# Three paddings in SBUF that move the operands of matrix products to multiples of 128 bytes

## The chip, the cores and the metric

The kernel is one program on one NeuronCore of a Trainium2 chip. The metric is the device time of one execution in microseconds, as the median of several runs. The engines are named as in the profile: PE (TensorE, matrix products; PEld is its loading of the stationary operand), DVE (VectorE), ACT (ScalarE), POOL (GpSimd) and SP (SyncE, which here only issues DMAs).

## The reference

One layer of a hybrid decoder: a token mixer with two parallel branches, then an MLP, both with RMS norm and residual, then a final RMS norm. The sequence has 1024 rows, the model width is 1024, all in float32. Cut to what matters:

```python
h = rms_norm(x, norm_mix)
xa, ga, q, f, v, g, m_a, m_b = split(h @ w_in)             # w_in: 1024 x 8192
xa = causal_depthwise_conv(xa, conv_w, conv_b)             # four taps
y_a = rg_lru(xa, w_r, b_r, w_i, b_i, lam) * gelu(ga)       # four blocks of 256 x 256 for each gate, then a scan
o = rms_norm(hgrn2_chunkwise(silu(q), k, log_f, v), hg_norm)   # 8 heads of 128
y = sigmoid(m_a) * y_a + sigmoid(m_b) * (o * silu(g))
x = x + y @ w_out                                          # 1024 x 1024
h = rms_norm(x, norm_mlp)
x = x + square(relu(h @ w_up)) @ w_down                    # 1024 x 4096, 4096 x 1024
out = rms_norm(x, norm_final)
```

## The kernel before

All large products run in fp32r, and each is made of three (`mm3`, L113): both operands are split into a high part H, rounded by ACT (L76), and the rest L, which DVE subtracts (L77); then H x H, H x L and L x H are accumulated in one PSUM bank. `PE.matmul(o, a, b)` takes `a` as the stationary operand (128 columns, loaded into the array) and `b` as the moving one (here up to 512 columns, read from SBUF while the product runs). In the profile's rows a product stands as `out<-moving,stationary`. L115, L116 and L117 are the three products of `mm3`.

The work goes in this order:

- Mixer. The sequence is cut into two halves of T = 512 rows (`c`), the width into four pairs of heads (`p`). For each of the 8 combinations: projections `v`, `xa`, `q`, `f`, `g`, `mb`, `ga`, `ma` (`project`, L270: 48 products of 512 columns with the normalised rows hT as the moving operand; `project_v`, L282: products of 256 columns with the weights moving); `conv` (L296), which writes the projection xa behind three carried columns into a tile `xp` and splits its result into xcH and xcL; `rg_lru` (L326) with 24 products per pair for its two gates, xcH and xcL moving; `hgrn` (L381), a chain of elementwise work on DVE with small fp32 products of 32, 48, 64 and 128 columns between; `gates` (L561). `out_proj` (L599) follows for the first half.
- Second norm (L686), with the output projection of the second half between its parts. Its results, in seven combinations (a scheme with seven instead of eight block products), are the tiles h2 (`hop`, L680): t1, n2, T3, T4, B11, B21, B22, each H and L.
- First half of the MLP (`hidden`, L804): 16 quads of 256 hidden columns, each in seven steps (`PLAN`) of 12 products of 512 columns, h2 moving, weights stationary. X, Y and Z are the banks that the steps accumulate into. ACT copies the bank of the first three steps out (L819), DVE and ACT finish the others (L822 to L827). The results u are split, combined, and most of them stored in HBM.
- Second half of the MLP (from L936): 8 rounds of two quads, 168 products of 512 columns per round. The weights move (the even quad from the pools w1 and wp, the odd one from late_w1 and late_w); the stationary operand is u (from ust and late_u). DVE adds the banks to the residual `acc` (L963). The last round is finished tile by tile with the final norm (`finish`, L917).

The order of instructions on each engine is fixed when the program is built; semaphores hold it. SBUF is handed out by pools: a pool takes its tiles one after the other, each rounded up to 32 bytes in a partition. Pools of the left side grow upwards from the small constants; those opened with `side="right"` grow downwards from the upper end: first `pad` (L673), one tile that nobody reads, then the four h2 pools, and, after these are closed, late_u, acc0, late_w, late_w1, late_raw and acc1. The mixer's pool `mix` lies on the left. Its tiles in order: the masks, scar, scT, g1, g2, on, xc, f, tmp, kT, v, then xp (two buffers, L300), xcH, xcL, q1, kk, h, rw, ri, rr, dd, seg, qa, hssq (two buffers, L518), sn and hrs. A tile that takes over bytes of a closed pool waits for the instructions that used the tile before.

Of the kernel before, what the change touches and what calls it, by code (L numbers as in the profile page):

```python
# [10 lines left out]
F32 = mybir.dt.float32  # L11
# [7 lines left out]
P = 128  # L19
D = 1024  # L20
S = 1024
T = 512
# [19 lines left out]
def trunk(ctx: ExitStack, tc: tile.TileContext, x, wts, mlp, pv, gains, mask_f, mask_u, out):  # L42
# [8 lines left out]
    def opened(name, **how):  # L51
        cm = tc.tile_pool(name=name, bufs=1, reuse_waits="tile", **how)
        return cm.__enter__(), lambda: cm.__exit__(None, None, None)
# [21 lines left out]
    def split(src, h, lo):  # L75
        keep(A.copy(h, src))  # L76
        keep(V.tensor_tensor(out=lo, in0=src, in1=h.bitcast(F32), op=ALU.subtract))  # L77
# [92 lines left out]
    def mt(tag, name, shape=(P, T), dt=F32, bufs=1):  # L170
        return m.tile(list(shape), dt, tag=tag, name=name, bufs=bufs)
# [98 lines left out]
    def project(c, name):  # L270

        pp = [bank("pj", f"pj_{name}_{s}") for s in range(2)]
        for half in range(2):
            wh, wl = next_w()
            for k in range(4):
                hh, hl = kt(hT[c], 4 * half + k)
                for s in range(2):
                    cols = slice(k * 256 + s * P, k * 256 + (s + 1) * P)
                    mm3(pp[s], wh[:, cols], wl[:, cols], hh, hl, half == 0 and k == 0, half == 1 and k == 3)
        return pp  # L280
# [15 lines left out]
    def conv(c, p, pp):  # L296
        xc = mt("xc", f"xc{c}{p}", (P, 2, T))
        for s in range(2):
            u = 2 * p + s
            xp = mt("xp", f"xp{c}{u}", (P, T + 3), bufs=2)  # L300
            V.tensor_copy(xp[:, 0:3], xcar[:, u, :])
            A.copy(xp[:, 3 : T + 3], pp[s])
            A.activation(
                xc[:, s, :],
                pp[s],
                AF.Identity,
                bias=pvt[:, PV_CB + u : PV_CB + u + 1],
                scale=pvt[:, PV_CW + 24 + u : PV_CW + 25 + u],
            )
            for j in range(3):  # L310
                V.scalar_tensor_tensor(  # L311
                    xc[:, s, :],
                    xp[:, j : j + T],
                    pvt[:, PV_CW + 8 * j + u : PV_CW + 8 * j + u + 1],
                    xc[:, s, :],
                    op0=ALU.mult,
                    op1=ALU.add,
                )
            if c + 1 < NC:
                G.tensor_copy(xcar[:, u, :], xp[:, T : T + 3])  # L320
        xh = mt("xcH", f"xcH{c}{p}", (P, 2, T), F32R)
        xl = mt("xcL", f"xcL{c}{p}", (P, 2, T), F32R)
        split(xc, xh, xl)
        return xc, xh, xl
# [43 lines left out]
    def f_of(c, p, pp):  # L368
        ff = mt("f", f"f{c}{p}", (P, 2 * T))
        kk = mt("kk", f"kk{c}{p}", (P, 2 * T))  # L370
        for s in range(2):
            u = 2 * p + s
            f, k = ff[:, s * T : (s + 1) * T], kk[:, s * T : (s + 1) * T]
            A.activation(f, pp[s], AF.Sigmoid)
            A.activation(k, pp[s], AF.Sigmoid, scale=-1.0)
            V.tensor_scalar(f, f, omlb[:, u : u + 1], lb[:, u : u + 1], op0=ALU.mult, op1=ALU.add)
            V.tensor_scalar(k, k, omlb[:, u : u + 1], None, op0=ALU.mult)
        V.tensor_scalar(ff, ff, F_MIN, 1.0, op0=ALU.max, op1=ALU.min)
        return ff, kk

    def hgrn(c, p, q1, f, kk, v):  # L381

        nm = f"{c}{p}"
# [131 lines left out]


        on = mt("on", f"on{nm}", (P, 8, P))
        ssq = mt("hssq", f"hssq{nm}", (P, 8), bufs=2)  # L518
        nkv = 3 if c + 1 == NC else 4
        pos = []  # L520
        for s in range(2):
            u = 2 * p + s
# [103 lines left out]
    for c in range(NC):  # L626
        if c == 0:
            first_norm(0)
            mu32 = small_inputs()
        else:  # L630
            out_proj(0, ys, res0, done0, lambda: first_norm(1))
        ys = a2_set(a2y, f"y{c}")
        for p in range(NPAIR):
            v = project_v(c, f"{c}{p}")
            px = project(c, f"xa{c}{p}")
            if c == 0 and p == 0:
                parameters()
                tc.keep_in_program_order(V.tensor_copy(mu, mu32.to_broadcast([P, 7, 8, 32])))
            xc3 = conv(c, p, px)
            q1 = q_of(c, p, project(c, f"q{c}{p}"))  # L640
            f, kk = f_of(c, p, project(c, f"f{c}{p}"))
            with tc.high_priority(300):
                h = rg_lru(c, p, *xc3)
            on = hgrn(c, p, q1, f, kk, v)
            gates(c, p, h, on, ys)
# [25 lines left out]


    pad, close_pad = opened("pad", side="right")  # L673
    pad.tile([P, 8], F32, tag="pad", name="pad")

    h2p = [opened(f"h2{i}", side="right") for i in range(4)]
    HOME = {"T4": 0, "B22": 0, "T3": 0, "B21": 1, "n2": 2, "t1": 2, "B11": 3}
# [371 lines left out]
```

## Time and profile before

| | before |
|---|---|
| median of 3 runs | 1631.38 us (1631.27 to 1631.52) |
| profiled execution | span 1628.7 us from the first to the last instruction; a time of its own beside the span is not recorded for it |
| median of the runs less the span | 2.7 us |
| PE busy | 1584.9 us, 97%, 9240 products |
| DVE busy | 1212.7 us, 74% |
| ACT busy | 764.4 us, 47% |
| mean granted TensorE clock | 0.996 |
| DMA | 246.51 MB, mean 151 GB/s |

How to read the profile: it is one execution. A row of the order of time has the start in us from the begin of the span, the duration in us, the engine, the line, the operation, and what it writes and reads; what stands in square brackets is how long the engine sat idle before, and who ended that. The printed durations of products overlap, since the next one starts while the last one still runs through the array; what a product costs in a dense row is the distance between two starts. A row of the waits names who waited for whom, the sum in us, how many times, and the longest.

### The profile page before, as it was taken

How to read it: one execution, taken by the hardware profiler on the slowest of the kernel's cores; microseconds unless marked ns; L12 is line 12 of the kernel's file. 1: busy time of each engine (PE TensorE's matmuls, PEld its weight loads, DVE VectorE, ACT ScalarE, POOL GpSimd, SP SyncE). 2: the span in 40 equal slices, each digit the busy share in tenths (PEclk: the TensorE clock that was granted, in tenths of full speed). 3: DMA queues.
4: the chain of work that ended last, by engine and by line, in shares of the span. 5: the costliest groups of instructions: out<-in, count | busy, mean ns of one | idle time of the engine just before them, and what ended most of it. 6: DMA issues, size and time to landing. Idle time of an engine off the chain costs nothing.

```text
span 1628.7 us, 23177 instructions
## 1 busy us (share of the span) xinstructions
PE 1584.9 (97%) x9240; PEld 1303.1 (80%) x9240; DVE 1212.7 (74%) x1751; ACT 764.4 (47%) x1186; POOL 65.8 (4%) x99
## 2 busy tenths in 40 slices
PE   7999999999999999999999997999999999999998
PEld 6788788788788788787787876888878878888886
DVE  5975956848764865848759688977777888888876
ACT  4643545435442544436434566766776731222113
POOL 0010100100100000100100100000000000000000
PEclk9999999999999999999999998999999999999999
DMA  6212212122243222222122352666656575666652
GB/s 237 91 66 91 91 66 103 66 91 91 80 167 136 86 78 90 80 78 101 69 91 91 117 207 104 250 246 250 235 233 248 222 269 228 251 244 251 254 203 104
DMA packets 57996, 246.51 MB, mean 151 GB/s; under 512 B 6688, under 2 KB 6816, under 8 KB 47136
## 3 DMA queue, kind: packets, MB, share of 16 engines
q1 hardware_dynamic: 56304, 239.27, 39.3%
q10 hardware_dynamic: 1584, 5.77, 1.0%
q8 instruction: 72, 1.18, 0.3%
q14 instruction: 36, 0.29, 0.1%
HBM read 185.24 MB, written 59.77 MB: 150 GB/s over the span
## 4 chain that ended last, share of the span: by engine, by line
PE 80%; DVE 16%; DMA 2%; issue 1%; ACT 1%; POOL 0%; DVEq 0%; POOLq 0%; SPq 0%; ACTq 0%
PE dX L115 3%; PE uX L115 3%; PE uX L117 3%; PE uX L116 3%; PE dX L116 3%; PE dX L117 3%; DVE wL L77 2%; PE pj_ga L117 2%; PE pj_ga L116 2%; PE pj_ga L115 2%; PE pj_f L117 2%; PE pv L115 2%; PE pv L117 2%; PE pv L116 2%; PE pj_ma L117 2%; PE pj_ma L116 2%
## 5 line engine op out<-in xcount | busy, mean ns | idle before, releaser
L77 DVE TENSOR_TENSOR wL<-raw,wH 128x1024 fp32r<-128x1024 f32 x160 | 194.3, 1214 | 150.0 <-ACT wH L76 145.8
L76 ACT CAST wH<-raw 128x1024 fp32r<-128x1024 f32 x160 | 167.9, 1050 | 168.1 <-issue 66.4
L963 DVE TENSOR_TENSOR acc<-acc,dX 128x512 f32<-128x512 f32 x128 | 85.2, 684 | 31.2 <-PE dX L117 30.1
L76 ACT CAST wA<-q 128x512 fp32r<-128x512 f32 x32 | 19.8, 621 | 129.6 <-PE dX L117 103.7
L963 DVE TENSOR_TENSOR acc<-acc,dY 128x512 f32<-128x512 f32 x64 | 43.6, 686 | 17.3 <-PE dY L117 15.7
L345 DVE RECIPROCAL rr<-rr 128x512 f32<-128x512 f32 x16 | 53.5, 3347 | 0.0
L823 ACT ACTIVATE b<-b 128x512 f32<-128x512 f32 x48 | 30.2, 631 | 38.6 <-DVE b L822 38.5
L115 PE MATMUL pv<-wH,hT0H 128*128 128x256 f32 x128 | 37.4, 292 | 0.0
L116 PE MATMUL pv<-wL,hT0H 128*128 128x256 f32 x128 | 37.0, 289 | 0.0
L117 PE MATMUL pv<-wH,hT0L 128*128 128x256 f32 x128 | 37.0, 289 | 0.0
L115 PE MATMUL pv<-wH,hT1H 128*128 128x256 f32 x128 | 36.5, 285 | 0.0
L117 PE MATMUL pv<-wH,hT1L 128*128 128x256 f32 x128 | 36.2, 283 | 0.0
L116 PE MATMUL pv<-wL,hT1H 128*128 128x256 f32 x128 | 36.2, 283 | 0.0
L311 DVE SCALAR_TENSOR_TENSOR xc<-xp,pvt,xc 128x512 f32<-128x512 f32 x48 | 33.1, 746 | 0.0
L551 ACT ACTIVATE on<-po 128x128 f32<-128x128 f32 x64 | 17.0, 278 | 33.5 <-PE po L541 33.2
L570 ACT ACTIVATE smb<-pj_mb 128x512 f32<-128x512 f32 x16 | 9.6, 598 | 45.3 <-PE pj_mb L117 45.2
L824 ACT ACTIVATE b<-b 128x512 f32<-128x512 f32 x48 | 30.1, 630 | 1.1
L77 DVE TENSOR_TENSOR wA<-q,wA 128x512 fp32r<-128x512 f32 x32 | 22.0, 687 | 9.9 <-ACT wA L76 9.7
L444 POOL TENSOR_SCALAR seg<-seg 128x128 f32<-128x128 f32 (+1 forms) x16 | 14.5, 905 | 361.1 <-DVE seg L384 361.1
L565 ACT ACTIVATE g<-pj_g 128x512 f32<-128x512 f32 x16 | 9.6, 600 | 37.2 <-PE pj_g L117 37.2
L384 DVE TENSOR_TENSOR seg<-seg 128x128 f32<-128x128 f32 (+2 forms) x96 | 26.7, 307 | 0.2
L117 PE MATMUL pj_ga<-hT1H,wL 128*128 128x512 f32 x64 | 26.5, 414 | 0.0
(1854 smaller groups left out, 5261.5 us busy)
## 6 DMA issues: line engine op xcount, KB each, us to landing
raw<-wts_in SPq DMA_DIRECT2D x160, 512.0 KB, 3.4
q<-mlp_in SPq DMA_DIRECT2D x64, 512.0 KB, 3.9
x<-x_in SPq DMA_DIRECT2D x8, 512.0 KB, 6.1
acc<-x ACTq DMA_DIRECT2D x8, 512.0 KB, 6.1
y_out<-acc SPq DMA_DIRECT2D x16, 256.0 KB, 2.1
xs<-x_in SPq DMA_DIRECT2D x8, 256.0 KB, 3.5
x<-xs SPq DMA_DIRECT2D x8, 256.0 KB, 2.3
x2s<-x_in SPq DMA_DIRECT2D x4, 512.0 KB, 4.7
```

The source lines that it names most:

```text
L76: keep(A.copy(h, src))
L77: keep(V.tensor_tensor(out=lo, in0=src, in1=h.bitcast(F32), op=ALU.subtract))
L115: PE.matmul(o, ah, bh, start=first, stop=False, **how)
L116: PE.matmul(o, ah, bl, start=False, stop=False, **how)
L117: PE.matmul(o, al, bh, start=False, stop=last, **how)
L311: V.scalar_tensor_tensor(xc[:, s, :], xp[:, j : j + T], pvt[:, PV_CW + 8 * j + u : PV_CW + 8 * j + u + 1], xc[:, s, :], op0=ALU.mult, op1= ...
L345: V.reciprocal(rec, rec)
L384: mul = lambda o, a, b: V.tensor_tensor(out=o, in0=a, in1=b, op=ALU.mult)
L551: A.activation(on[:, 4 * s + n, :], po[:, n * P : (n + 1) * P], AF.Square, accum_out=ssq[:, 4 * s + n : 4 * s + n + 1])
L823: A.activation(b[:, at, :], b[:, at, :], AF.Relu, scale=-1.0 if at == 2 else 1.0)
L824: A.activation(b[:, at, :], b[:, at, :], AF.Square)
L963: V.tensor_tensor(out=dst, in0=dst, in1=banks[bk, pr], op=op)
```

## The change

Three tiles get larger; nothing else is changed. `xp` has 528 columns instead of 515, `ssq` is the first eight columns of a tile of 16, and the unused tile at the right end has 24 columns instead of 8.

```diff
@@ -297,7 +297,7 @@
         xc = mt("xc", f"xc{c}{p}", (P, 2, T))
         for s in range(2):
             u = 2 * p + s
-            xp = mt("xp", f"xp{c}{u}", (P, T + 3), bufs=2)
+            xp = mt("xp", f"xp{c}{u}", (P, T + 16), bufs=2)
             V.tensor_copy(xp[:, 0:3], xcar[:, u, :])
             A.copy(xp[:, 3 : T + 3], pp[s])
             A.activation(
@@ -515,7 +515,7 @@
 
 
         on = mt("on", f"on{nm}", (P, 8, P))
-        ssq = mt("hssq", f"hssq{nm}", (P, 8), bufs=2)
+        ssq = mt("hssq", f"hssq{nm}", (P, 16), bufs=2)[:, 0:8]
         nkv = 3 if c + 1 == NC else 4
         pos = []
         for s in range(2):
@@ -671,7 +671,7 @@
 
 
     pad, close_pad = opened("pad", side="right")
-    pad.tile([P, 8], F32, tag="pad", name="pad")
+    pad.tile([P, 24], F32, tag="pad", name="pad")
 
     h2p = [opened(f"h2{i}", side="right") for i in range(4)]
     HOME = {"T4": 0, "B22": 0, "T3": 0, "B21": 1, "n2": 2, "t1": 2, "B11": 3}
```

## The prediction

> **What bounds the kernel now.** I read the page from the top: the engines' shares, then the chain that ended last.
>
> ```profile
> span 1628.7 us, 23177 instructions
> ## 1 busy us (share of the span) xinstructions
> PE 1584.9 (97%) x9240; PEld 1303.1 (80%) x9240; DVE 1212.7 (74%) x1751; ACT 764.4 (47%) x1186; POOL 65.8 (4%) x99
> ...
> PE 80%; DVE 16%; DMA 2%; issue 1%; ACT 1%; POOL 0%; DVEq 0%; POOLq 0%; SPq 0%; ACTq 0%
> ```
>
> The matrix engine is busy for 97% of the span and holds 80% of the chain; so whatever shortens one product, times the number of products, shortens the kernel, except where the vector engine (16% of the chain) sets the pace. A busy PE says nothing about how fast each product runs, so the next view is the order of time, PE alone, and in it the distance between two starts, not the printed duration (the products overlap).
>
> The addresses I worked out from the tile sizes in the code, each rounded up to 32 bytes in the order in which the pools hand them out. A multiple of 128 at present: hT, y, v, the weight tiles w and w1, the state tiles sn. 64 bytes past a multiple: in the mixer all that is allocated behind xp (two buffers of 2060 bytes, which take 2080 each), so xcH and xcL; and all that is allocated from the right end behind the pad of 32 bytes, so the four h2 pools, late_w1, late_w and late_u. First a stretch in which both operands are at multiples of 128, a projection of 48 products:
>
> ```profile
> 40.57 0.39 PE L115 MATMUL pj_q<-hT0H,wH 128*128 128x512 f32 x1
> ...
> 51.45 0.39 PE L115 MATMUL pj_f<-hT0H,wH 128*128 128x512 f32 x1
> ```
>
> 10.88 us over 48 is 226.7 ns from start to start. The same shape with a moving operand 64 bytes off, once in the gate products of the RG-LRU (18 products from the first row to the second) and once in the MLP's first half (five steps of 12, so 60 products):
>
> ```profile
> 55.68 0.40 PE L115 MATMUL pi<-xcH,wH 128*128 128x512 f32 x1
> ...
> 59.88 0.39 PE L117 MATMUL pj_f<-hT0H,wL 128*128 128x512 f32 x1
> ```
>
> ```profile
> 1089.98 0.39 PE L115 MATMUL uX<-h2T4H,wA124H 128*128 128x512 f32 x1
> ...
> 1103.98 0.39 PE L115 MATMUL uX<-h2T3H,ws35H 128*128 128x512 f32 x1
> ```
>
> 4.20 us over 18 and 14.00 us over 60: 233.3 ns both times. Same shape, same three-product scheme, the two stretches a thousand microseconds apart in different surroundings: 6.67 ns more per product where the moving address is 64 bytes off. That is the quantity that the change can remove.
>
> **The change part by part.** It adds no instruction, takes none away and moves none: the program's order, its waits and its DMAs stay. What changes is addresses. xp grows by 32 bytes in each of two buffers, so all mixer tiles behind it move up by 64; ssq grows to 64 bytes in each of two buffers, which moves sn by 64 more, and so leaves sn at a multiple of 128; the pad grows by 64 bytes, so every tile on the right side moves down by 64. Not all moving operands become multiples: the small score products take slices of q1, qa and qb every 192, 224 or 8 + 224 bytes, and keep their mixture. Their terms I set at nothing.
>
> *Growth of the right pad, MLP's first half (`hidden`).* 16 quads of 7 steps of 12 products are 1344 products, all with h2 as the moving operand. 1344 x 6.67 ns = 8.96 us. Two parts of it I don't count. The first quad is fed by other engines:
>
> ```profile
> PE xT_h L704 <- DVE rstd_h L137: 6.2, 2, 5.5
> PE sc L394 <- DVE qb L384: 5.0, 8, 0.6
> PE sc L394 <- DVE q L384: 4.0, 8, 0.5
> ...
> PE uX L115 <- ACT ws30H L76: 1.7, 1, 1.7
> ```
>
> In the fourth of these rows a product of the first quad waits for the split of its weights; faster products before it only wait longer. 84 x 6.67 = 0.56 us off. Second, every other quad from the fifth has a small wait at step T3, seen in the order of time:
>
> ```profile
> 1081.49 1.05 ACT L76 CAST ws15H<-s 128x1024 fp32r<-128x1024 f32 x1 [1.98 <-PE uX L116]
> ...
> 1084.35 0.58 ACT L819 COPY e<-uX 128x512 f32<-128x512 f32 x1
> ```
>
> ```profile
> 1085.02 0.46 PE L115 MATMUL uX<-h2T3H,ws34H 128*128 128x512 f32 x1
> 1085.32 0.39 PE L116 MATMUL uX<-h2T3L,ws34H 128*128 128x512 f32 x1
> ...
> 1281.29 0.45 PE L115 MATMUL uX<-h2T3H,ws314H 128*128 128x512 f32 x1
> ```
>
> ScalarE is released by the products of step n2, does three casts and then the copy that empties bank X; the copy ends at 1084.93 and the next product into that bank starts at 1085.02, with 0.30 us to its successor and not 0.233. The casts and the copy keep their length, while the 15 products that lie between (Z's 12 and 3 of Y's) become 0.10 us shorter; so the wait grows by 0.10 us in the six quads from the first of these rows to the last: 0.6 us off. In the quads between, the steps come in another order, T3 right behind Z:
>
> ```profile
> 1102.62 0.57 ACT L819 COPY e<-uX 128x512 f32<-128x512 f32 x1
> ```
>
> This copy is done at 1103.19, 0.79 us before T3's first product at 1103.98 (a row above), which leaves room for the 0.08 us by which Z's 12 products shrink. Left: 7.8 us.
>
> *The same growth, MLP's second half.* Here half of the 1344 products take the moving weights from w and w1 (at 0), half from late_w and late_w1 (at 64), changing after every six. One round of 168 products, and inside it a stretch of six from the late side:
>
> ```profile
> 1388.01 0.39 PE L115 MATMUL dX<-wA,u2B 128*128 128x512 f32 x1
> ...
> 1397.67 0.39 PE L115 MATMUL dZ<-wA1219H,u3B 128*128 128x512 f32 x1
> ...
> 1399.03 0.39 PE L115 MATMUL dX<-ws318H,u2n 128*128 128x512 f32 x1
> ...
> 1426.70 0.39 PE L115 MATMUL dX<-wA,u4B 128*128 128x512 f32 x1
> ```
>
> 38.69 us over 168 is 230.3 ns: about halfway between 226.7 and 233.3, as the moving address alone would have it. But the six products between the second and third row, with the moving operand at 64, run at 1.36 / 6 = 226.7 ns. Their stationary operand (late_u) is at 64 too, whereas in `hidden` and the RG-LRU the stationary one is at 0. So it may be that the two addresses must agree modulo 128, and that what costs here is the change of sides. Either reading ends at the same place, since after the change both operands are at 0 throughout: 1344 x 3.63 = 4.9 us. The surroundings:
>
> ```profile
> 1311.00:1354.00 43.00, 42.29 (x182) 33.42 (x181) 37.70 (x55) 13.81 (x17) 0.00 (x0) 1.00 0.77 294
> ...
> 1392.00:1431.00 39.00, 39.00 (x171) 31.79 (x170) 31.47 (x46) 7.56 (x8) 0.00 (x0) 1.00 0.62 247
> ```
>
> The columns are the stretch, the busy time of PE, PEld, DVE, ACT and POOL with counts, the granted clock, the DMA share and GB/s. In the steady state DVE has 31.5 us of work in 39.0 and the DMA engines are at 0.62, so a round that is 0.6 us shorter still covers both. In the first 43 us PE is not full, DVE is at 88% and the DMAs at 0.77: 182 products x 3.63 = 0.7 us I count as swallowed, and 0.1 us at the very end, where the last additions lead. Left: 4.1 us.
>
> *Growth of xp, the RG-LRU's gate products.* 8 pairs x 24 = 192 products x 6.67 = 1.28 us at most, nothing at least. What waits there is DVE:
>
> ```profile
> 164.89 0.43 DVE L342 TENSOR_SCALAR rw<-rw 128x512 f32<-128x512 f32 x1 [2.17 <-ACT rw L338]
> ```
>
> From this instruction DVE works almost without a gap until PE waits for it twice per pair (the second and third rows of the waits above, 9.0 us in 16 waits). It starts as soon as the first six of the 24 products are through. So six count and the other 18 turn into longer waits: 8 x 6 x 6.67 = 0.3 us.
>
> *Growth of ssq.* It keeps sn where it was modulo 128; without it sn would be at 64. Zero.
>
> *Projections that are cut up by small products.* Some rows of the page stand above their neighbours:
>
> ```profile
> L117 PE MATMUL pj_ga<-hT1H,wL 128*128 128x512 f32 x64 | 26.5, 414 | 0.0
> ```
>
> In the undisturbed projection above the printed duration is 0.39 us, here it is 414 ns, although hT and w are at 0. These products stand behind the small fp32 products, whose stationary operands (kk, qf) move from 64 to 0. If 10 of these 25 ns went for all 384 of this projection, it would be 3.8 us; I take nothing, since a switch between kinds of product is the nearer cause, and keep a part for the range.
>
> Sum: 7.8 + 4.1 + 0.3 = 12.2 us of the profiled span of 1628.7. The median of the runs, 1631.38, is 2.7 us above that span, and this remainder I leave as it is: 1631.4 - 12.2 = **1619.2 us**.
>
> **The rivals.** *The second half gains nothing* because its 230.3 ns comes from its own pattern (the stationary tile changes every three products). For it: the six late products at 226.7 ns show that the address alone isn't the whole rule. Against it: the output projection has the same pattern with all operands at 0, 66 products between these rows, 226.8 ns:
>
> ```profile
> 450.15 0.39 PE L115 MATMUL po<-wH,y0H 128*128 128x512 f32 x1
> ...
> 465.12 0.39 PE L115 MATMUL po<-wH,y0H 128*128 128x512 f32 x1
> ```
>
> Time: 1631.4 - 7.8 - 0.3 = 1623.3 us.
>
> *No address matters.* Then 233.3 ns would come from accumulating long in one bank (12 products in a row in `hidden`, 6 in the gates, 3 in the projections). Against it: the v projection puts 24 in a row into one bank, 256 columns each, 42 products between these rows:
>
> ```profile
> 128.28 0.28 PE L115 MATMUL pv<-wH,hT0H 128*128 128x256 f32 x1
> ...
> 133.32 0.28 PE L115 MATMUL pv<-wH,hT0H 128*128 128x256 f32 x1
> ```
>
> That is 120.0 ns; the 256 further columns of 226.7 cost 106.7, so 13.3 ns stay per product in both, and nothing extra for the long row. Time: 1631.4 us. The Trainium skill says the same as this rival in another way: TensorE: Matmul & The Clock Gate, section "Back-to-back issue gap", gives the distance as a function of columns and clock alone, and SBUF — State Buffer, section "Specifications (TRN2)", names lines of 16 bytes, of which 64 bytes are four whole ones; by both this change gives nothing. The trace has two distances at the same columns and the same clock, so it does not agree with the first.
>
> *Slower.* Pools here reuse bytes of closed pools, and a first write waits for the last reader of each tile that it overlaps. If a moved boundary made h2 tiles overlap a mixer tile that is read late, the second norm would wait at each such tile, as it does now for rstd_h: longest 5.5 us in the first of the waits above. From three such waits (16.5 us) on it outweighs the 12.2: 1635.7 us. Against it: shifting the tiles by the amounts above, I find the same pairs of overlapping tiles as before.
>
> **How the numbers follow.** The forecast has 0.77, the second half gaining nothing 0.12, no effect of addresses 0.06, slower 0.05. The range: below, all terms in full (8.96 + 4.9 + 1.28 = 15.1, so 1616.3) and some 2 us of the cut-up projections: 1614.5; above, the first rival and another 1.2 us of `hidden` lost to waits of the T3 kind: 1624.5. About 0.2%, 3.3 us, is what a measurement of this kernel can tell from no change. Both first cases lie beyond it: faster 0.89; same 0.06; slower 0.05.
>
> **What would show it.** Right: in `hidden` starts 226.7 ns apart, a quad of 84 products at 19.04 us plus the T3 wait, and this wait at about 0.16 us in six quads; in the second half 226.7 ns and a round of 168 at 38.1 us; the gate products at 226.7 ns, with the waits of sc for qb and q grown together by about 1 us. Wrong: 233 ns or more in `hidden`; a round in the second half still at 38.7 us; new waits at the second norm; DVE or DMA as the releaser of products in the steady rounds of the second half.

## The result, and the profile after

The changed kernel takes 1626.64 us (median of 9 runs, 1625.44 to 1628.68); the kernel before, on the same chip, 1631.27 (9 runs, 1629.61 to 1631.72). The ratio is 0.9973 with a 95% interval of 0.9964 to 0.9982. So the change gains 4.6 us, where 12.2 were forecast and 1624.5 was the upper end of the range. The order of the instructions on every engine is the same as before. The head of the page, after:

```profile
span 1625.8 us, 23177 instructions
...
PE 1583.0 (97%) x9240; PEld 1306.5 (80%) x9240; DVE 1212.2 (75%) x1751; ACT 764.6 (47%) x1186; POOL 65.0 (4%) x99
...
PE 80%; DVE 15%; DMA 2%; issue 1%; ACT 1%; POOL 0%; DVEq 0%; POOLq 0%; SPq 0%; ACTq 0%
```

The profiled execution is 2.9 us shorter than that of before (1628.7), where the medians differ by 4.6. In the runs for which both are recorded, the time is 1.7 to 1.9 us above the span. By these, the profiled execution of before is estimated at 1630.5 us, some 0.8 below its median, and that of after (1627.60) is 1.0 above its own. Now the three stretches of the prediction in the order of time, PE alone; first the gates' 18 products, then 60 of `hidden`:

```profile
55.65 0.39 PE L115 MATMUL pi<-xcH,wH 128*128 128x512 f32 x1
...
59.73 0.39 PE L117 MATMUL pj_f<-hT0H,wL 128*128 128x512 f32 x1
```

```profile
1088.22 0.40 PE L115 MATMUL uX<-h2T4H,wA124H 128*128 128x512 f32 x1
...
1102.17 0.39 PE L115 MATMUL uX<-h2T3H,ws35H 128*128 128x512 f32 x1
```

The gates are at 4.08 / 18 = 226.7 ns from start to start, as forecast. `hidden` is at 13.95 / 60 = 232.5 ns, hardly less than the 233.3 of before, although its moving operand is now at a multiple of 128. One round of 168 products in the second half:

```profile
1387.09 0.39 PE L115 MATMUL dX<-wA,u2B 128*128 128x512 f32 x1
...
1425.43 0.39 PE L115 MATMUL dX<-wA,u4B 128*128 128x512 f32 x1
```

38.34 us, or 228.2 ns per product: between the 38.69 of before and the 38.1 forecast. The surroundings, the same stretches and columns as before:

```profile
1311.00:1354.00 43.00, 41.26 (x175) 32.34 (x174) 36.77 (x53) 12.29 (x16) 0.00 (x0) 1.00 0.76 293
1392.00:1431.00 39.00, 39.00 (x173) 32.18 (x172) 31.81 (x46) 7.57 (x8) 0.00 (x0) 1.00 0.63 250
```

In the first of these stretches PE was busy for 1 us less (41.26 us instead of 42.29). Where the time went shows best in the starts of the same four products, taken from the order of time of each version (us; the other kernels are explained below):

| | first of `hidden` | first of the second half | its second round | last product |
|---|---|---|---|---|
| before | 988.51 | 1305.85 | 1348.91 | 1620.71 |
| after | 987.05 | 1303.76 | 1348.20 | 1617.93 |
| pad of 56 | 987.42 | 1299.43 | 1342.29 | 1610.18 |
| left side moved by 128 | 986.82 | 1297.51 | 1341.23 | 1609.13 |
| pad of 24 alone | 988.38 | 1304.87 | 1347.91 | 1617.61 |
| pad of 56 alone | 989.00 | 1299.69 | 1343.29 | 1611.12 |
| xp and ssq alone | 988.01 | 1305.33 | 1348.86 | 1620.71 |

From before to after: the part up to `hidden` gains 1.46 us, `hidden` 0.63, the later rounds of the second half 2.07; the first round gives 1.38 back.

### The profile page after: what moved, and what is told of

Read it like the earlier page. It is cut to its first block, busy times and chain, and to the rows that moved or that the text cites. A ratio compares the mean times of both kernels' runs of the same rounds, so it can differ in the third digit from the quotient of the medians.

```text
span 1625.8 us, 23177 instructions
## 1 busy us (share of the span) xinstructions
PE 1583.0 (97%) x9240; PEld 1306.5 (80%) x9240; DVE 1212.2 (75%) x1751; ACT 764.6 (47%) x1186; POOL 65.0 (4%) x99
## 4 chain that ended last, share of the span: by engine, by line
PE 80%; DVE 15%; DMA 2%; issue 1%; ACT 1%; POOL 0%; DVEq 0%; POOLq 0%; SPq 0%; ACTq 0%
PE uX L115 3%; PE uX L117 3%; PE dX L115 3%; PE uX L116 3%; PE dX L117 3%; PE dX L116 3%; DVE wL L77 2%; PE pj_ga L117 2%; PE pv L116 2%; PE pv L117 2%; PE pv L115 2%; PE pj_ga L115 2%; PE pj_ga L116 2%; PE pj_f L117 2%; PE pj_ma L115 2%; PE pj_ma L117 2%
```

## The theories

The addresses in the prediction were worked out modulo 128. Modulo 256 there is more to see. (They follow from the tile sizes and stand in no profile; what the runs can test is how far two operands lie apart.) In both kernels the weights w that `hidden` loads as its stationary operand lie at 0, and hT at 0. h2 lay at 192 before and lies at 128 after; xcH went from 192 to 0. In the second half the odd quad has both its operands on the right side (late_w and late_u), the even quad both on the left.

- **R**: what counts is the distance, moving less stationary address, modulo 256. At 0 a product takes 226.7 ns, at other distances up to 234. `hidden` went from 192 to 128, both of which cost; only the gates reached 0.
- **M**: the moving address alone counts, and it must be a multiple of 256.
- **B**: no address rule in `hidden`; its 232.5 ns come from 12 products in a row into one PSUM bank.

By the trace of the changed kernel alone all three could be true.

## The experiments

**Pad of 56 columns** instead of 24, so that the right side goes down by 128 more and h2 lies at 0:

```diff
-    pad.tile([P, 24], F32, tag="pad", name="pad")
+    pad.tile([P, 56], F32, tag="pad", name="pad")
```

> As the changed kernel, but the unused tile at the right end has 56 columns instead of 24, which moves everything on the right side down by another 128 bytes: h2, late_u, late_w and late_w1 then lie at multiples of 256, like the weight tiles w and w1. Theory R (what costs is the distance between the moving and the stationary address modulo 256; 0 is free, in the first half of the MLP the changed kernel left it at 128): starts in hidden 226.7 ns apart instead of 232 to 233, second half of the MLP 226.7 ns without the steps of 230 and 233 ns at each change of side; 1344 x 5.8 = 7.8 us and 1344 x 1.67 = 2.2 us less, some of it lost to the waits of step T3: 1617 us. Theory M (the moving address alone has to be a multiple of 256): the same in hidden; in the second half too. Rival B (twelve products in a row into one bank cost 6 ns each, no address matters there): hidden stays at 232 to 233 ns, total 1625 to 1627 us.

Measured: 1619.96 us (5 runs, 1618.97 to 1620.53), ratio to before 0.9933 (0.992 to 0.9945). The same rows of `hidden` and of the round:

```profile
1088.25 0.39 PE L115 MATMUL uX<-h2T4H,wA124H 128*128 128x512 f32 x1
...
1101.85 0.39 PE L115 MATMUL uX<-h2T3H,ws35H 128*128 128x512 f32 x1
```

```profile
1380.94 0.39 PE L115 MATMUL dX<-wA,u2B 128*128 128x512 f32 x1
...
1419.02 0.39 PE L115 MATMUL dX<-wA,u4B 128*128 128x512 f32 x1
```

13.60 / 60 and 38.08 / 168: 226.7 ns both times. B falls, since the banks are used as before. R and M both fit, and so the next kernel.

**Left side moved by 128.** The changed kernel with its pad of 24, and one unused tile of 128 bytes at the head of the left side. Everything on the left moves from 0 to 128; h2 stays at 128:

```diff
+    const.tile([P, 32], F32, tag="shift", name="shift")
```

> As the changed kernel, with an unused tile of 128 bytes among the constants: everything on the left side (weights, hT, the mixer's tiles, ust) moves up by 128 bytes and so leaves the multiples of 256, the right side stays where it was, 128 bytes off a multiple of 256. R: the two operands agree modulo 256 everywhere: hidden 226.7 ns, second half 226.7 ns, the projections keep their 226.7 ns; 1617 us as with the larger pad. M: no moving operand is at a multiple of 256 any more: hidden stays at 232 to 233 ns and the 3264 large products of the mixer and the output projections rise to 232 ns too: 1640 us or more. B: nothing changes, 1626.6 us.

Measured: 1619.05 us (5 runs, 1618.55 to 1620.72), ratio 0.9931 (0.9917 to 0.9944). `hidden`, and the round:

```profile
1086.38 0.39 PE L115 MATMUL uX<-h2T4H,wA124H 128*128 128x512 f32 x1
...
1099.98 0.39 PE L115 MATMUL uX<-h2T3H,ws35H 128*128 128x512 f32 x1
```

```profile
1379.84 0.39 PE L115 MATMUL dX<-wA,u2B 128*128 128x512 f32 x1
...
1417.92 0.39 PE L115 MATMUL dX<-wA,u4B 128*128 128x512 f32 x1
```

Again 13.60 and 38.08 us, with no moving operand of `hidden` at a multiple of 256. The projections, whose two operands moved together, keep their 226.7 ns (the 384 products of pj_q: 226.66 on average). M falls, R stands: moving the stationary operand towards the moving one does the same as the reverse.

**Other distances.** Unused tiles of 8 columns in the first three h2 pools of the changed kernel put its seven operands at four distances: T4, T3 and B22 at 128, B21 at 96, t1 and n2 at 64, B11 at 32.

```diff
+    for i, n in enumerate((8, 8, 8)):
+        h2p[i][0].tile([P, n], F32, tag="step", name=f"step{i}")
```

> As the changed kernel, with an unused tile of 32 bytes in each of three of the h2 pools, so that the steps of hidden see four distances to the weights modulo 256: T3, T4 and B22 at 128, B21 at 96, t1 and n2 at 64, B11 at 32. R and M: each distance has its own spacing of starts, above 226.7 ns for all of them, 232 to 233 at 128. B: all steps alike.

One run: 1628.73 us. One quad, the first product of each step of 12:

```profile
1090.47 0.39 PE L115 MATMUL uX<-h2T4H,wA124H 128*128 128x512 f32 x1
...
1093.26 0.39 PE L115 MATMUL uX<-h2B11H,wA 128*128 128x512 f32 x1
...
1096.06 0.39 PE L115 MATMUL uY<-h2t1H,ws15H 128*128 128x512 f32 x1
...
1098.81 0.39 PE L115 MATMUL uX<-h2n2H,ws15H 128*128 128x512 f32 x1
...
1101.55 0.40 PE L115 MATMUL uZ<-h2B21H,wA125H 128*128 128x512 f32 x1
...
1104.37 0.40 PE L115 MATMUL uX<-h2T3H,ws35H 128*128 128x512 f32 x1
```

A step takes 2.79 us at 128, 2.80 at 32, 2.75 and 2.74 at 64, 2.82 at 96. None is at the 2.72 of distance 0. But the cost isn't even: 64 is the cheapest of them.

**The other side, and the period.** With the pad of 56 and tiles of 8, 16 and 40 columns: T4, T3 and B22 at 0, B21 at 224, t1 and n2 at 160, and B11 at 256, which is 0 if the period is 256 but not if it is 512.

```diff
-    pad.tile([P, 24], F32, tag="pad", name="pad")
+    pad.tile([P, 56], F32, tag="pad", name="pad")
...
+    for i, n in enumerate((8, 16, 40)):
+        h2p[i][0].tile([P, n], F32, tag="step", name=f"step{i}")
```

> Pad of 56 columns (as in the version with all distances at 0) and unused tiles of 8, 16 and 40 columns at the head of the first, second and third h2 pools. Distance of the moving from the stationary operand, modulo 256: T4, B22 and T3 at 0, B21 at 224, n2 and t1 at 160, B11 at 0 (but at 256 modulo 512). Theory R (distance modulo 256): 226.7 ns from start to start in T4, B22, T3 and B11, more than 228 in B21, n2 and t1. Its variant with period 512: B11 at 232 to 234. Theory 'multiples of 128 of the moving address': T4, B22, T3 and B11 at 226.7, only B21, n2 and t1 above, like R; this run alone does not separate these two. From the distances already measured (128: 233, 96: 234, 64: 229, 32: 233) 224 mirrors 32 and 160 mirrors 96: if the cost is symmetric, 233 and 234. Time 1619.96 + 16 quads x 36 products x 6.6 ns = about 1623.8 us, with the longer period 1625.

One run: 1620.7 us.

```profile
1087.28 0.39 PE L115 MATMUL uX<-h2T4H,wA124H 128*128 128x512 f32 x1
...
1090.00 0.39 PE L115 MATMUL uX<-h2B11H,wA 128*128 128x512 f32 x1
...
1092.72 0.40 PE L115 MATMUL uY<-h2t1H,ws15H 128*128 128x512 f32 x1
...
1095.52 0.40 PE L115 MATMUL uX<-h2n2H,ws15H 128*128 128x512 f32 x1
...
1098.33 0.40 PE L115 MATMUL uZ<-h2B21H,wA125H 128*128 128x512 f32 x1
...
1101.13 0.40 PE L115 MATMUL uX<-h2T3H,ws35H 128*128 128x512 f32 x1
```

B11 takes 2.72 us like T4: so 256 is as good as 0, and 128 is not: the period is 256. Means over all the quads (spacings under 260 ns, so without waits):

| distance | 0 | 32 | 64 | 96 | 128 | 160 | 192 | 224 | 256 |
|---|---|---|---|---|---|---|---|---|---|
| ns per product | 226.7 to 227.0 (T3 228.7) | 233.3 | 228.9 to 229.5 | 234.2 | 232.8 to 233.2 | 233.8 to 234.2 | 233.3 | 233.3 | 226.7 |

(192 is the kernel before; T3 at 0 has the T3 wait in it. In all columns but that of 0 the stationary operand stayed where it was and the moving one was shifted.) The expected symmetry holds for 32 and 224 and for 96 and 160, but not for 64 and 192. The time came out 3 us lower than expected. The extra cost per round in `hidden` is about as priced: from the third round on this kernel gains about 0.55 us per round on the kernel before, the pad of 56 about 0.97. What differs is the way in: the pad of 56 lost 0.80 us on before in the first 168 products of `hidden` (which wait for ScalarE and DVE), this one gained 0.24, and was 0.6 us ahead at their start: 1.6 of the 3 us. And one thing more differs in both kernels with unused tiles in the h2 pools: the order of 91 matrix products around the passage to the second half is another than in all other kernels here (in the last quad T3 comes ahead of B22). The spacings above come from steps that this does not touch, but the two times can't be compared with the others as if only addresses had changed. Such differences of a microsecond between single executions set the limit for reading spans here.

**xp and ssq alone**: the gates at distance 0, the rest as before. Against the changed kernel:

```diff
-    pad.tile([P, 24], F32, tag="pad", name="pad")
+    pad.tile([P, 8], F32, tag="pad", name="pad")
```

> The pad is back at 8 columns, xp and ssq keep their growth: the mixer's part of the change alone. R and M: gate products 226.7 to 227 ns, everything up to the second norm 1.5 us earlier, hidden at 233.3 ns and the second half at 230.3 ns as in the kernel before: 1629.8 us. B: the gates have six products in a row into one bank and should be slow again (233 ns), total as before.

Measured: 1629.71 us (11 runs, 1628.3 to 1631.29) against 1630.76, ratio 0.9993 (0.9984 to 1.0002), not to be told from no change by itself. In the trace its lead over before grows to 0.73 us over the first four of the mixer's eight pairs, as in the changed kernel (0.72), but 0.5 of it goes at the passage to the second half of the sequence and 0.3 more at the second norm. `hidden` stays at 233.3 ns.

**The pad of 24 alone** (xp and ssq as before):

```diff
-            xp = mt("xp", f"xp{c}{u}", (P, T + 16), bufs=2)
+            xp = mt("xp", f"xp{c}{u}", (P, T + 3), bufs=2)
...
-        ssq = mt("hssq", f"hssq{nm}", (P, 16), bufs=2)[:, 0:8]
+        ssq = mt("hssq", f"hssq{nm}", (P, 8), bufs=2)
```

> The right pad alone grows from 8 to 24 columns; xp and ssq stay as they were. The changed kernel took 1626.64. If the gate products bring the 1.5 us that the trace of the changed kernel shows ahead of hidden: 1628.1 us. If they bring 0.3 as predicted: 1626.9. In either case gates at 233.3 ns, hidden at 232 to 233, second half at 228.3.

Measured: 1628.3 us (10 runs, 1626.98 to 1632.68), ratio 0.9985 (0.9976 to 0.9994). So xp and ssq bring 1.7 us by the medians; in the traces `hidden` starts 988.38 - 987.05 = 1.33 us later without them.

**The pad of 56 alone**: xp and ssq undone as in the last diff, and the pad with

```diff
-    pad.tile([P, 24], F32, tag="pad", name="pad")
+    pad.tile([P, 56], F32, tag="pad", name="pad")
```

> The right pad alone grows from 8 to 56 columns, so that the distance is 0 modulo 256 in both halves of the MLP; xp and ssq stay as they were. With the growth of xp and ssq it took 1619.96. If the gates are worth 1.5 us: 1621.5. If 0.3: 1620.3. Hidden and second half at 226.7 to 227.2 ns, gates at 233.3.

Measured: 1620.83 us (4 runs, 1620.74 to 1621.2), ratio 0.9938 (0.9921 to 0.9954). Here the difference is 0.9 us by the medians and 989.00 - 987.42 = 1.58 by the traces. So the growth of xp and ssq is worth 0.9 to 1.7 us.

**The pad of 56 without the growth of ssq**, with that of xp:

```diff
-        ssq = mt("hssq", f"hssq{nm}", (P, 16), bufs=2)[:, 0:8]
+        ssq = mt("hssq", f"hssq{nm}", (P, 8), bufs=2)
```

> Pad of 56 columns and the growth of xp, without that of ssq; the state tiles sn then lie 64 bytes past a multiple of 256. Prediction's view: ssq's growth is worth nothing, so 1619 to 1621 us as with it (1619.96) and the mixer ends within 0.2 us of that version. Rival: the products that read sn also pay for a distance of 64 modulo 256; then the mixer ends 0.3 us or more later and their spacing grows.

One run: 1620.61 us. The mixer ends 0.25 us later than with it, 0.10 of which is there before the first product that reads sn, and the products that read sn keep their spacing. With ssq's growth the same tiles lie at 128 modulo 256, so the run compares 64 with 128, and neither with 0. The 96 products that read sn take 10.31 to 10.35 us from start to start in all ten traces. Prediction and rival are too close for one execution's total; nothing speaks for a cost.

## Why the prediction was wrong, point by point

**The quantity.** This is the step that failed: "6.67 ns more per product where the moving address is 64 bytes off. That is the quantity that the change can remove." The 6.67 ns are real, and so are the three places that show them. But they belong to a pair of addresses, of a moving and a stationary operand, with a period of 256, and in all three places the stationary address was a multiple of 256, so that moving address and distance looked alike. After the change the moving address of `hidden` was a multiple of 128, but 128 from the stationary one, and its products took 232.5 ns; at distance 0, reached from either side, they take 226.7. The row that contradicted it was noticed, the six late products at 226.7 ns, and so was its reading, that "the two addresses must agree modulo 128". Then came "Either reading ends at the same place, since after the change both operands are at 0 throughout". That holds modulo 128 only, and no row said that 128 was the period. The tiles' addresses were at hand to 32 bytes: modulo 256 they show h2 at 128 and w at 0 after the change, and the question would have been open.

**Term 1, `hidden`: 7.8 us forecast, 0.63 measured.** The distance went from 192 to 128, and 233.3 ns to 232.8 on average. With distance 0 the term is 5.3 us (pad of 56) and about 6.6 (left side moved, and pad of 56 alone), from the differences of the first two columns of the table. So the sum was too high even for the mechanism that it assumed. Of the first round of 168 products nothing much comes through (I counted 84 as lost), and with distance 0 the T3 wait grew as expected in the six quads, from 0.30 us to

```profile
1083.05 0.39 PE L117 MATMUL uY<-h2B22H,ws34L 128*128 128x512 f32 x1
1083.33 0.50 PE L115 MATMUL uX<-h2T3H,ws34H 128*128 128x512 f32 x1
1083.67 0.40 PE L116 MATMUL uX<-h2T3L,ws34H 128*128 128x512 f32 x1
```

in the version with the pad of 56 (0.28 + 0.34 for two starts that were 0.23 + 0.30 apart before: 0.1 us), while two longer ones, 0.3 us more in one of the six and 0.3 in the last quad, were not in the forecast.

**Term 2, second half: 4.1 us forecast, 2.07 in the later rounds, less 1.38 in the first.** With distance 0 and no change of side the later rounds gain 3.9 to 4.0 us in all three versions of that kind, and with the first round 4.1, 3.2 and 3.4. The forecast's size was right for the state that the change did not reach. In the changed kernel both operands of a product are at 0 or both at 128, so the distance is 0 always; yet the first and the last product of a row of six on one side take 230.5 and 232.5 ns on average, those between 226.8. The change of side itself costs. A round has 28 rows of six and 26 changes of side (twice two rows of one side follow one another). By the rounds, 38.34 - 38.08 = 0.26 us is 10 ns for each change when the sides are 128 apart; 38.69 - 38.08 = 0.61 us is 23 ns for each when they were 192 apart, where the cost is spread over the row. This also fits the six at 226.7 in the prediction: they follow six others of the same side.

Which operands meet at a change can be read from the profile after, where the loading of the stationary operand (PEld) has rows of its own:

```profile
1427.94 0.40 PE L117 MATMUL dX<-wA,u5B 128*128 128x512 f32 x1
1427.94 0.19 PEld L115 LDWEIGHTS dY<-ws120H,u4t 128*128 128x128 f32 x1
1428.17 0.39 PE L115 MATMUL dY<-ws120H,u4t 128*128 128x512 f32 x1
```

The first row is the last product of six on the right side; while it runs, the stationary operand of the next product is loaded, and that one lies on the left, 128 away. The 232.5 ns of such a product are those of `hidden` at 128 (232.8). So the pair that counts may be a product's moving operand and the next product's stationary one. In `hidden`, where all weights lie at 0, both readings give the same, and no run separates them. Not explained by this are the 3.8 ns of a row's first product and the larger, spread cost at 192. The kernel before shows that a cost can outlast its cause: behind the gates (moving operand at 192) the first three to eleven products of pj_f have both operands at 0, and still take up to 237 ns, 20 or 43 ns more together than in the kernel after.

**The first round.** PE was 2.1 us ahead at its begin and 0.7 at its end. Not the forecast's 0.7 us of swallowed gain, but a loss. A weight tile is issued on SP's queue, cast on ACT, and subtracted on DVE, which stands still for it; before, after, and with the pad of 56:

```profile
1330.19 0.94 SPq L747 DMA_DIRECT2D q<-mlp_in  x2
...
1340.52 0.62 ACT L76 CAST wA<-q 128x512 fp32r<-128x512 f32 x1 [16.76 <-DMA q<-mlp_in]
...
1341.17 0.69 DVE L77 TENSOR_TENSOR wA<-q,wA 128x512 fp32r<-128x512 f32 x1 [2.44 <-ACT wA L76]
```

```profile
1328.50 1.07 SPq L747 DMA_DIRECT2D q<-mlp_in  x2
...
1339.85 0.62 ACT L76 CAST wA<-q 128x512 fp32r<-128x512 f32 x1 [17.81 <-DMA q<-mlp_in]
...
1340.50 0.69 DVE L77 TENSOR_TENSOR wA<-q,wA 128x512 fp32r<-128x512 f32 x1 [3.43 <-ACT wA L76]
```

```profile
1323.74 1.04 SPq L747 DMA_DIRECT2D q<-mlp_in  x2
...
1333.98 0.62 ACT L76 CAST wA<-q 128x512 fp32r<-128x512 f32 x1 [16.57 <-PE dY L116]
```

Issued 1.69 us earlier, it is cast only 0.67 earlier: from the issue 10.33 us before, 11.35 after, at most 10.24 with the pad of 56 (there the cast was held last by PE). The pad of 24 alone, with the same addresses on the right side, has 10.32 (1329.23 to 1339.55) and loses nothing in that round (43.04 us from the first product of the second half to the second round, 43.06 before, 44.44 after). So the loss isn't a property of the right side's addresses; the profiled execution of the changed kernel had a slower transfer there. In the eight kernels with the same order of instructions the round follows this time from issue to cast:

| | issue to cast, us | first round, us |
|---|---|---|
| pad of 56 | 10.24 | 42.86 |
| pad of 24 alone | 10.32 | 43.04 |
| before | 10.33 | 43.06 |
| pad of 56, without the growth of ssq | 10.57 | 43.52 |
| xp and ssq alone | 10.61 | 43.53 |
| pad of 56 alone | 10.90 | 43.60 |
| left side moved by 128 | 11.00 | 43.72 |
| after | 11.35 | 44.44 |

(With the pad of 56, and with xp and ssq alone, it was a matrix product that released the cast last.) What made the transfer slower was not tried.

**Term 3, the gates: 0.3 us forecast, 0.9 to 1.7 by the medians, 1.3 by the traces**, which is the 1.28 that stood as the maximum. From start to start the 192 gate products take 46.22 us before and 45.22 after, and pj_f, whose products stand between and behind them, 88.37 and 88.10. The two together are 134.58 to 134.59 us in the three kernels without the growth of xp and 133.32 to 133.37 in the seven with it. The step that failed is "six count and the other 18 turn into longer waits". The waits of sc did not grow:

```profile
PE sc L394 <- DVE qb L384: 5.0, 8, 0.6
PE sc L394 <- DVE q L384: 4.0, 8, 0.5
```

DVE's chain restarts in its middle. Before and after:

```profile
174.90 0.43 DVE L342 TENSOR_SCALAR rw<-rw 128x512 f32<-128x512 f32 x1 [0.19 <-ACT rw L338]
```

```profile
174.54 0.43 DVE L342 TENSOR_SCALAR rw<-rw 128x512 f32<-128x512 f32 x1
```

```profile
171.05 1.06 ACT L76 CAST wH<-raw 128x1024 fp32r<-128x1024 f32 x1 [2.62 <-PE pj_f L116]
```

```profile
170.69 1.06 ACT L76 CAST wH<-raw 128x1024 fp32r<-128x1024 f32 x1 [2.54 <-PE pj_f L116]
```

ACT's cast of the next weights waits for a product of pj_f, which stands behind all 24 gate products; ACT's next sigmoid, and so DVE's second half of the chain, come after that cast. Both cast and DVE are 0.36 us earlier, as much as PE's lead at the end of this pair. The row of 174.90 stands ten rows below the one at which the prediction stopped reading this chain.

**What was counted as nothing.** ssq, as above. The projections that are cut up by small products keep their duration (414 ns for pj_ga's line, before and after), although the small products' operands kk and qf moved from 192 to 0 against w; so this move is not worth anything there. The small fp32 products for sc take 33.01 to 33.02 us from start to start in all ten traces; both their operands lie behind xp and move together.

**The rivals.** "The second half gains nothing" did not come, nor did the new waits of the fourth rival. "No address matters" is refuted by 128 unused bytes on the left that are worth 7.6 us beside the changed kernel (1619.05 against 1626.64). The Trainium skill, TensorE: Matmul & The Clock Gate, section "Back-to-back issue gap", gives the distance without the addresses; the traces don't agree, since here 512 columns at the granted clock of 0.996 take 226.7 to 234.2 ns by addresses alone. The Trainium skill, SBUF — State Buffer, section "A bandwidth-pool intuition that's wrong (but worth ruling out)", gives PE a second, independent read port for loading weights; the runs show that the place of the stationary operand has a part in the time of dense products (232.5 against 226.7 ns in `hidden` when only the left side was moved).

## The version that is faster than both

The pad of 56 columns with the grown xp and ssq (1619.96 us), and the changed kernel with 128 unused bytes at the head of the left side (1619.05 us): ratios of 0.9933 and 0.9931 to before. Their intervals overlap almost wholly. The forecast of 1619.2 us is close to what the change would have given with the right side 128 bytes lower. That closeness is in part luck: with the pad of 56 `hidden` gave 5.3 us where 7.8 were forecast, the part ahead of it 1.1 where 0.3 were, and the second half 4.1 as forecast.

## What to carry to other kernels

Where dense matrix products differ by a few ns per product at the same shape and clock, tabulate the addresses of both operands, and their distance, at several moduli before naming a rule; a rule that three stretches support may only mean that the other operand never moved. Test it by moving the other operand: one unused tile at the head of a pool does it. Then compare the order of instructions with that of the kernel before, because an unused tile can change that too, as in two of the kernels here. And follow a chain of waits past its first restart before you say that an engine hides a gain.

## What the runs showed of the hardware that was not expected

- In dense fp32r products of 128 x 128 by 512 columns (granted clock 0.996), the address of the moving less that of the stationary operand modulo 256 goes with the distance from start to start: 226.7 ns at 0, 228.9 to 229.5 at 64, 232.8 to 234.2 at 32, 96, 128, 160, 192 and 224. That it is the pair was tested by moving either operand to distance 0; the other distances were made by shifting the moving operand alone.
- A change of side by both operands, to one 128 bytes off, costs about 10 ns, to one 192 off about 23, although the distance within each product stays at 0.
- By the profile the stationary operand is loaded while the product ahead runs (1427.94 us, above), so the pair that counts may be that of one product's moving and the next one's stationary operand. This, why 64 is cheaper than 192, and why the cost can outlast the change of address by up to eleven products, stays open.
